# The opening of a diffusion layer on one core: the silu columns as a transfer of their own, another order of TensorE's first products, and one block of the third group moved by a place

## The chip, the core and the metric

The kernel runs on one core of one Trainium2 chip. The metric is the device time of one execution in microseconds (us); of the kernel before there are three runs, and their median stands for it.

## What is computed

One layer of a diffusion backbone, for 256 latent tokens with a prefix of 256 context tokens, width 2048, all in F32. What matters here is the first step, in which shift and scale come from a conditioning vector (`c` for the latent tokens, `c_ctx` for the context):

```python
def rms_norm(x, g):
    y = xf * lax.rsqrt(jnp.mean(xf * xf, axis=-1, keepdims=True) + EPS)
    return y * g
def modulate(x, g, shift, scale):
    return rms_norm(x, g) * (1 + scale) + shift
...
mod_x = jnp.split(jax.nn.silu(c) @ w_mod + b_mod, 6, axis=-1)
mod_c = jnp.split(jax.nn.silu(c_ctx) @ w_mod + b_mod, 6, axis=-1)
...proj(modulate(x, g_mix, mod_x[0], mod_x[1]))    # h @ w_in: the input projection
...proj(modulate(ctx, g_mix, mod_c[0], mod_c[1]))
```

Then follow windowed attention and a gated linear attention side by side, their merge, and a convolutional feed-forward; the change does not touch them.

## The kernel before

The projections multiply F32 by splitting each weight block into a high and a low part: ScalarE (ACT) copies the high part (`whi`, line 211), VectorE (DVE) takes the difference (`wlo`, line 212), and TensorE (PE) adds three products. The modulated tokens are split in the same way (`h00hi`, `h00lo` for the latent ones, `h10hi`, `h10lo` for the context).

The 16 tiles of 128 channels are worked in five groups (`GROUPS`: 2, 2, 4, 4 and 4 tiles), so that the projection can begin before the whole modulation is known. For each group, `mod_both` (line 312) makes the scale columns and then the shift columns: PE multiplies `cS`, the silu of the conditioning columns, with blocks of 1 MB of the modulation matrix (`pm <- mraw, cS`); DVE transposes the result (`mtr`); PE folds it into columns (`pcol <- mtr`), and DVE copies it out and adds the bias (lines 345 and 348). `affine_scale` and `affine_shift` apply the columns to the tokens.

The opening is a row of calls (lines 537 to 594). The constants come in two transfers on ACT's queue: `pack` (the identity matrix `ident`, biases, norm weights, the selector `sel` and, in its last 32 columns, both conditioning vectors), and `crow`. SP's queue loads the tokens (`xT`, two of 1 MB), the first group's four blocks, the first weights (`w_first`, four of 512 KB), the context tokens, and so on. `square_sums` squares the tokens on ACT and DVE, and PE adds them up over the channels with a matrix of ones (`pr <- sq, ones`: nine products, called by `add_up`). `factor_row` makes the norm's factors from that, three steps on DVE with two on ACT between. `idle(n)` issues n transposes of the identity matrix (`warm <- pack`), whose result nobody reads. `pe_seq` chains PE's instructions of the opening in the order of the calls.

The third group's blocks are worked among the second group's products. Six places are named by `mid()`: ahead of the second half of the latent QB projection, in its middle, behind it, in the middle of the KB projection, behind it, and in the middle of the VB projection. `steps` says how many blocks go to each place, `also` what else is done there, and `pend` holds the folding into columns that follows the last block of a kind. `kb` and `vb` are the sums of these projections over the groups, which DVE adds up from PE's banks (line 521).

PE's order follows the calls. On the other engines a scheduler places instructions by its own estimate of when they are ready. Each engine works in order.

## Time and profile before

| what | value |
|---|---|
| median of 3 runs | 1973.95 us (1973.88 to 1974.18) |
| the profiled execution's own time | 1973.72 us |
| its span, from the first instruction to the last | 1972.0 us |
| TensorE busy | 1952.8 us (99%) |
| VectorE busy | 1396.9 us (71%) |
| ScalarE busy | 971.6 us (49%) |
| DMA queue of SP | 413.45 MB, 63.7% of 16 engines' span |
| granted TensorE clock | 1.00 throughout |

A row of the timeline gives the start and the duration in us, the engine, the line, the operation, the tile that is written and the ones read, the shape and a count; in brackets stands how long the engine had been idle, and what ended that. SPq and ACTq are the queues that issue transfers. L83 and L95 are the helpers through which nearly all matmuls are issued, so the names of the tiles tell them apart.

### The profile page before, as it was taken

Reading aid. Unit: us, or ns where it says so; the run is one execution under the profiler, and the core shown is the slowest. Engines: PE = TensorE matmul, PEld = TensorE weight load, DVE = VectorE, ACT = ScalarE, POOL = GpSimd, SP = SyncE. Lnnn points to the kernel's source line nnn. Section 1 sums busy time; section 2 is a strip of 40 time slices with the busy share of each in tenths; the row PEclk is TensorE's granted clock in tenths of the full one; section 3 lists DMA queues with packets and bytes.
Section 4 is the critical chain, followed back from the end, with each engine's and each line's share of the span. In section 5 each row is a group of like instructions: output and inputs, shape, how many; then the busy total and the mean of one; then the engine's idle time right before and its main releaser. Section 6 shows DMA issues by size and latency. Waiting matters only on the chain.

```text
span 1972.0 us, 27091 instructions
## 1 busy us (share of the span) xinstructions
PE 1952.8 (99%) x10304; PEld 1635.6 (83%) x10304; DVE 1396.9 (71%) x2150; ACT 971.6 (49%) x1415; POOL 39.9 (2%) x60
## 2 busy tenths in 40 slices
PE   8999999999999999999999999999999999999999
PEld 6679988888887777888888888888888888888887
DVE  5756855785768998777776467989886545677754
ACT  5223655462346565444444445755555334555533
POOL 0010000020000000000000000000000000000000
PEclk9999999999999999999999999999999999999999
DMA  9975222226654466899997677688786556666563
GB/s 392 412 255 176 69 66 71 79 84 210 212 162 126 129 208 220 297 299 307 312 310 237 238 246 252 193 276 284 263 275 224 192 193 191 186 188 191 188 212 114
DMA packets 182867, 420.90 MB, mean 213 GB/s; under 512 B 12512, under 2 KB 12736, under 8 KB 177744
## 3 DMA queue, kind: packets, MB, share of 16 engines
q1 hardware_dynamic: 181200, 413.45, 63.7%
q0 software_dynamic: 1360, 5.54, 1.0%
q8 instruction: 81, 1.33, 0.3%
q14 instruction: 50, 0.41, 0.1%
q10 hardware_dynamic: 176, 0.17, 0.0%
HBM read 416.98 MB, written 2.13 MB: 213 GB/s over the span
## 4 chain that ended last, share of the span: by engine, by line
PE 94%; DVE 3%; ACT 1%; DMA 1%; issue 1%; ACTq 0%; DVEq 0%
PE acc L83 72%; PE accs L83 12%; PE pa L95 2%; PE poa L95 1%; PE pS L95 1%; PE po L95 1%; PE pm L95 1%; DVE wlo L212 1%; PE ptp L98 1%; DMA mraw<-in_w_mod 1%; ACT whi L211 0%; DVE q L831 0%; PE pto L98 0%; DMA pack<-in_k_pack 0%; DVE k L838 0%
## 5 line engine op out<-in xcount | busy, mean ns | idle before, releaser
L212 DVE TENSOR_TENSOR wlo<-raw,whi 128x1024 fp32r<-128x1024 f32 x568 | 694.0, 1223 | 426.5 <-ACT whi L211 387.8
L211 ACT ACTIVATE whi<-raw 128x1024 fp32r<-128x1024 f32 x568 | 601.1, 1059 | 785.1 <-PE acc L83 605.0
L83 PE MATMUL accs<-h,whi 128*128 128x512 f32 x704 | 176.3, 392 | 0.0
L83 PE MATMUL acc<-h,whi 128*128 128x512 f32 x640 | 160.4, 392 | 0.0
L83 PEld LDWEIGHTS accs<-h,whi 128*128 128x128 f32 x704 | 126.6, 189 | 22.6
L83 PE MATMUL acc<-whi,h01hi 128*128 128x512 f32 x352 | 139.7, 397 | 0.0
L83 PE MATMUL acc<-whi,h00hi 128*128 128x512 f32 x352 | 139.2, 395 | 0.0
L83 PE MATMUL acc<-whi,h01lo 128*128 128x512 f32 x352 | 138.4, 393 | 0.0
L83 PE MATMUL acc<-whi,h00lo 128*128 128x512 f32 x352 | 137.6, 391 | 0.0
L83 PE MATMUL acc<-whi,al 128*128 128x512 f32 x352 | 137.0, 389 | 0.0
L83 PE MATMUL acc<-whi,ah 128*128 128x512 f32 x352 | 137.0, 389 | 0.0
L83 PEld LDWEIGHTS acc<-h,whi 128*128 128x128 f32 x640 | 115.1, 189 | 20.6
L83 PEld LDWEIGHTS accs<-h,wlo 128*128 128x128 f32 x704 | 96.0, 190 | 6.9
L83 PE MATMUL acc<-wlo,h01hi 128*128 128x512 f32 x352 | 99.0, 396 | 0.0
L83 PE MATMUL accs<-h,wlo 128*128 128x256 f32 x704 | 98.2, 282 | 0.0
L83 PE MATMUL acc<-wlo,h00hi 128*128 128x512 f32 x352 | 98.1, 394 | 0.0
L83 PE MATMUL acc<-wlo,ah 128*128 128x512 f32 x352 | 94.3, 389 | 0.0
L83 PEld LDWEIGHTS acc<-h,wlo 128*128 128x128 f32 x640 | 87.4, 190 | 6.3
L83 PE MATMUL acc<-h,wlo 128*128 128x256 f32 x640 | 89.4, 282 | 0.0
L376 DVE CUSTOM_DVE_ANT_0 raw<-raw,csrow,pack 128x1024 f32<-128x1024 f32 x64 | 81.2, 1278 | 0.0
L83 PEld LDWEIGHTS acc<-whi,al 128*128 128x128 f32 x352 | 66.1, 188 | 13.7
L83 PEld LDWEIGHTS acc<-whi,ah 128*128 128x128 f32 x352 | 66.1, 188 | 13.7
(376 smaller groups left out, 3553.0 us busy)
## 6 DMA issues: line engine op xcount, KB each, us to landing
raw<-in_w_in SPq DMA_DIRECT2D x204, 512.0 KB, 4.5
raw<-in_w_up SPq DMA_DIRECT2D x176, 512.0 KB, 4.2
raw<-in_w_modT SPq DMA_DIRECT2D x128, 512.0 KB, 4.6
raw<-in_w_down SPq DMA_DIRECT2D x88, 512.0 KB, 3.6
mraw<-in_w_mod SPq DMA_DIRECT2D x30, 1024.0 KB, 12.5
raw<-in_w_attn_o SPq DMA_DIRECT2D x32, 512.0 KB, 5.3
raw<-in_w_gla_o SPq DMA_DIRECT2D x32, 512.0 KB, 5.4
raw<-in_w_out SPq DMA_DIRECT2D x32, 512.0 KB, 4.4
```

The costliest lines, as they stand in the source:

```text
L83: r = pe_seq(PE.matmul(*a, **k))
L95: return pe_seq(after(PE.matmul(*a, **k)))
L98: return pe_seq(after(PE.transpose(*a)))
L211: j = S.activation(hi[:, 0:n, :], raw[:, 0:n, :], AF.Copy).ins
L212: i = V.tensor_tensor(lo[:, 0:n, :], raw[:, 0:n, :], hi[:, 0:n, :].bitcast(F32), op=ALU.subtract).ins
L376: i0 = V.tensor_tensor_reduce(out=raws[i], in0=raws[i], in1=row[0], scale=1.0, scalar=d if h else bmod[:, b0:b0 + 1], op0=ALU.mult, op1=AL ...
```

## The change

It has five parts. The conditioning columns leave `pack` and become a transfer of their own, `ccol`, first in ACT's queue; `pack` goes behind `crow`. The opening has fewer idle transposes, and the first scale block (`a0`) goes ahead of the last three sums of squares. The last shift block of the first and the second group is loaded whole, no longer in halves. DVE's `gm1` is put behind the first square. Of the third group's four shift blocks three stay at the fourth place, and one goes to the fifth; its columns are folded at the sixth.

```diff
-    pack = cst.tile([P, 322], F32, name="pack")
-    nc.scalar.dma_start(pack, A["k_pack"])
+    ccol = cst.tile([P, KT, 2], F32, name="ccol")
+    nc.scalar.dma_start(ccol.rearrange("p k s -> p (k s)"), A["k_ccol"])
     crow = sm.tile([KT, P], F32, name="crow", tag="t128", bufs=2)
     nc.scalar.dma_start(crow, A["k_crow"])
+    pack = cst.tile([P, 290], F32, name="pack")
+    nc.scalar.dma_start(pack, A["k_pack"])
...
-    S.activation(cS[:, :, 0:2], pack[:, 290:322].rearrange("p (k s) -> p k s", s=2), AF.Silu)
+    S.activation(cS[:, :, 0:2], ccol, AF.Silu)
...
-            src = A["w_mod01"][part, t0 + k0 // nk].rearrange("p (c d) -> p c d", c=nk)
-            if t0 < 4 and part == 0 and k0:
-                load(raw[:, 0:nk // 2, :], src[:, 0:nk // 2, :])
-                load(raw[:, nk // 2:nk, :], src[:, nk // 2:nk, :])
-            else:
-                load(raw, src)
+            load(raw, A["w_mod01"][part, t0 + k0 // nk].rearrange("p (c d) -> p c d", c=nk))
...
-    idle(10)
+    idle(8)
     pr, add_up = square_sums(0)
     add_up(0, 6)
-    V.tensor_scalar(gm1, gmix, -0.5, None, op0=ALU.mult)
+    in_order(squared[0], V.tensor_scalar(gm1, gmix, -0.5, None, op0=ALU.mult).ins)
     (a0, a1, ea), (b0, b1, eb) = mods[0]
+    a0()
     add_up(6, 9)
     factor_row(pr)
-    a0()
-    idle(6)
     a1()
-    idle(4)
+    idle(2)
     ea()
     b0()
     affine_scale(0, *groups[0])
-    idle(6)
+    idle(4)
     b1()
...
-                steps = iter([1, 2, 1, 4, 0, 0])
+                steps = iter([1, 2, 1, 3, 1, 0])
...
-                also = iter([next_columns] * 3 + [scale_2, next_columns, lambda: affine_shift(0, *groups[2])])
+                def shift_2():
+                    next_columns()
+                    affine_shift(0, *groups[2])
+
+                also = iter([next_columns] * 3 + [scale_2, next_columns, shift_2])
```

The start of ACT's queue before, from the program's first row on (`ACT_TABLE_LOAD` loads the table for silu, then the one for logarithm and exponential):

```order
L116 DMA pack<-in_k_pack 128x322
L118 DMA crow<-in_k_crow 16x128
L133 ACT_TABLE_LOAD
L133 ACTIVATE cS<-pack 128x16x2
L134 ACTIVATE crow<-crow 16x128
```

And with the change:

```order
L116 DMA ccol<-in_k_ccol 128x32
L118 DMA crow<-in_k_crow 16x128
L120 DMA pack<-in_k_pack 128x290
L135 ACT_TABLE_LOAD
L135 ACTIVATE cS<-ccol 128x16x2
L136 ACTIVATE crow<-crow 16x128
```

The transfer that PE's first instruction reads, pack, has moved from the first place to the third; ccol has as many rows as pack had.

PE's opening before, up to the last idle transposes (`pm1` are scale products, `pm0` shift products):

```order
L538 MATMUL warm_109<-pack_81 128x128
L535 MATMUL warm_109<-pack_81 128x128 x10
L462 MATMUL pr_121<-sq_122,ones_91 128x256 x4
L462 MATMUL pr_121<-sq_124,ones_91 128x256 x2
L462 MATMUL pr_121<-sq_127,ones_91 128x256
L462 MATMUL pr_121<-sq_131,ones_91 128x256 x2
L95 MATMUL pm1_0_152<-mraw_153,cS_93 32x256 x8
L535 MATMUL warm_109<-pack_81 128x128 x6
L95 MATMUL pm1_0_152<-mraw_169,cS_93 32x256 x8
L535 MATMUL warm_109<-pack_81 128x128 x4
L95 MATMUL pcol1_0_185<-mtr_179,pack_81 32x16
L95 MATMUL pm0_0_192<-mraw_193,cS_93 32x256 x8
```

And with the change:

```order
L537 MATMUL warm_111<-pack_85 128x128
L534 MATMUL warm_111<-pack_85 128x128 x8
L461 MATMUL pr_121<-sq_122,ones_93 128x256 x4
L461 MATMUL pr_121<-sq_124,ones_93 128x256 x2
L95 MATMUL pm1_0_141<-mraw_142,cS_95 32x256 x8
L461 MATMUL pr_121<-sq_127,ones_93 128x256
L461 MATMUL pr_121<-sq_131,ones_93 128x256 x2
L95 MATMUL pm1_0_141<-mraw_163,cS_95 32x256 x8
L534 MATMUL warm_111<-pack_85 128x128 x2
L95 MATMUL pcol1_0_177<-mtr_173,pack_85 32x16
L95 MATMUL pm0_0_184<-mraw_185,cS_95 32x256 x8
```

The first scale block has moved ahead of the last three sums; behind the second scale block two idle transposes are left of four, and between the scale blocks none. Behind these rows stand four idle transposes instead of six, then the last shift block, as before.

DVE around the third group's shift columns before, from the scaling of the context tokens on:

```order
L502 SCALAR_TENSOR_TENSOR xr_87<-xr_87,scale_102,rrow 128x256 x4
L335 STREAM_TRANSPOSE mtr<-pm_4_693 128x512
L521 TENSOR_TENSOR kb_107<-kb_107,acc 128x512 x4
L345 COPY shift_101<-pcol_4_740 32x2x4 x4
L348 TENSOR_TENSOR shift_101<-shift_101,pack 128x2x4
L212 TENSOR_TENSOR wlo<-raw,whi 128x1024
L512 SCALAR_TENSOR_TENSOR h00lo<-xr_85,shift_101,h00hi 128x256 x4
L521 TENSOR_TENSOR vb_108<-vb_108,acc 128x512 x4
```

And with the change:

```order
L501 SCALAR_TENSOR_TENSOR xr_89<-xr_89,scale_104,rrow 128x256 x4
L520 TENSOR_TENSOR kb_109<-kb_109,acc 128x512 x4
L332 STREAM_TRANSPOSE mtr<-pm_4_681 128x512
L342 COPY shift_103<-pcol_4_752 32x2x4 x4
L520 TENSOR_TENSOR vb_110<-vb_110,acc 128x512
L214 TENSOR_TENSOR wlo<-raw,whi 128x1024
L345 TENSOR_TENSOR shift_103<-shift_103,pack 128x2x4
L520 TENSOR_TENSOR vb_110<-vb_110,acc 128x512
L511 SCALAR_TENSOR_TENSOR h00lo<-xr_87,shift_103,h00hi 128x256 x4
L520 TENSOR_TENSOR vb_110<-vb_110,acc 128x512 x2
```

The transpose has moved behind the kb evictions, and between the copies of the shift columns and their bias add (L348 before, L345 now) stand a vb eviction and a weight split; one more eviction stands ahead of h00lo.

More of the change, by code (lines that the diff above doesn't have):

```diff
@@ L429, in layer_kernel @@
     vb0 = M("vb0", [P, 4, 512])
+    squared = []
     def square_sums(s):
@@ L442, in square_sums @@
             else:
-                V.tensor_tensor(q, x_, x_, op=ALU.mult)
+                squared.append(V.tensor_tensor(q, x_, x_, op=ALU.mult).ins)
                 parts.extend(q[:, k, :] for k in range(4))
@@ L1348 @@
         [consts.pop("k_ident")] + [col(data.pop(n)[0]) for n in ("b_mod", "g_mix", "g_ffn")]
-        + [consts.pop("k_sel"), np.stack([col(c), col(c_ctx)], axis=2).reshape(P, 2 * KT)], axis=1)
+        + [consts.pop("k_sel")], axis=1)
+    data["k_ccol"] = np.stack([col(c), col(c_ctx)], axis=2).reshape(P, 2 * KT)
     conv = data.pop("conv_w")[0]
```

## The prediction

> **What bounds the kernel now.** I read the page first, then the waits of TensorE (PE), then the order of time in two short stretches. The page says that there is almost nothing to gain: PE is busy for all but 19.2 us of the span, and the chain that ended last is PE for 94%.

> ```profile
> span 1972.0 us, 27091 instructions
> PE 1952.8 (99%) x10304; PEld 1635.6 (83%) x10304; DVE 1396.9 (71%) x2150; ACT 971.6 (49%) x1415; POOL 39.9 (2%) x60
> PE 94%; DVE 3%; ACT 1%; DMA 1%; issue 1%; ACTq 0%; DVEq 0%
> ```

> Who kept PE waiting, longest in total first (us in total, times, longest):

> ```profile
> PE warm L538 <- DMA pack<-in_k_pack: 6.7, 1, 6.7
> PE pm L95 <- DMA mraw<-in_w_mod: 1.2, 1, 1.2
> ```

> So PE's two waits on transfers are the wait for the constants at the start (6.7) and one wait for a block of the modulation matrix (1.2). The change touches both. Beside them the opening holds padding: "warm" transposes that compute nothing and count as busy. The opening in order of time, PE only (start, duration, operation; a matmul of 256 columns in F32 stands as two records):

> ```profile
> 6.68 0.47 PE L538 MATMUL warm<-pack 128*128 128x128 f32 x1 [6.68 <-DMA pack<-in_k_pack]
> 6.95 2.34 PE L535 MATMUL warm<-pack 128*128 128x128 f32 x10
> 9.08 3.63 PE L462 MATMUL pr<-sq,ones 128*128 128x256 f32 x12
> 13.07 1.64 PE L462 MATMUL pr<-sq,ones 128*128 128x256 f32 x6 [0.37 <-DVE sq L453]
> 14.64 1.07 PE L95 MATMUL pm<-mraw,cS 128*32 128x256 f32 x16
> 19.14 0.87 PE L535 MATMUL warm<-pack 128*128 128x128 f32 x6
> 19.94 1.07 PE L95 MATMUL pm<-mraw,cS 128*32 128x256 f32 x16
> 20.94 0.66 PE L535 MATMUL warm<-pack 128*128 128x128 f32 x4
> 23.30 0.39 PE L83 MATMUL acc<-h00hi,whi 128*128 128x256 f32 x1 [0.46 <-ACT h00hi L511]
> ```

> The first real product starts at 23.30; from there PE hardly stops, so a shift of that moment reaches the end unless a later wait swallows it. The last shift block is the 512 KB load of this row, issued in the stretch 6.6 to 7.0 us:

> ```profile
> mraw<-in_w_mod SPq DMA_DIRECT2D x1, 512.0 KB, 12.8
> ```

> It lands at about 19.5. Its products started only at 19.94, since six warm transposes stood ahead (19.14 to 20.0). From that start to the first product are 3.36 us (19.94 to 23.30).

> **The change, part 1: the opening.** With four warm transposes in place of six the last block's products could start on landing, and the first product come at 19.5 + 3.36 = 22.9, **0.4 earlier**. That holds only if PE gets there in time, and PE's very first instruction reads pack. Pack was first in ACT's queue and is now third. These are its issue and that of crow, the landing times (us from issue), and the packets that each queue started between 3 and 5 us (q1 is SP's queue, q10 ACT's; two rows of the queue table, then ACT's):

> ```profile
> q1 hardware_dynamic: 82, 0.67, 80.1%
> q10 hardware_dynamic: 82, 0.11, 16.0%
> ```

> ```profile
> 0.74 0.41 ACTq L116 DMA_DIRECT2D pack<-in_k_pack  x1
> 1.18 0.45 ACTq L118 DMA_DIRECT2D crow<-in_k_crow  x1
> ```

> ```profile
> pack<-in_k_pack ACTq DMA_DIRECT2D x1, 161.0 KB, 5.9
> crow<-in_k_crow ACTq DMA_DIRECT2D x1, 8.0 KB, 5.9
> ```

> 82 against 82: the engines serve the two queues one packet each in turn, whatever the size. 82 turns on 16 engines in 2.0 us make 0.39 us a turn, nearly all of it SP's packet. Pack has 128 rows, 8 turns on each engine; so has ccol, although it is a tenth of the size. I therefore put ccol where pack was, a little sooner for its smaller packets (a packet of pack takes 16.0% x 16 x 2.0 / 82 = 0.06, so 8 of them save 0.5 at most; I take 0.3): 6.3 instead of 6.6. Crow landed 0.5 after pack (1.18 + 5.9 against 0.74 + 5.9) and keeps that: 6.8. Pack then needs 8 turns of its own, 3.1: **9.9**, 3.2 later than now. Bounds: 7.1, when crow landed as the last of the same bytes, if bytes decide and not turns; and 10.5 with nothing saved on ccol and one more turn to close. I take 9.9, since the row comes from this very queue beside this very stream.

> [...]

> Now PE from 9.9 on. Nine warm transposes by the two rows (0.27, then 0.213 each): 2.0, until 11.9. Six sums of squares are 12 records. Their weight loads tell the speed:

> ```profile
> 8.87 2.16 PEld L462 LDWEIGHTS pr<-sq,ones 128*128 128x128 f32 x8
> 11.57 0.73 PEld L462 LDWEIGHTS pr<-sq,ones 128*128 128x128 f32 x4 [0.55 <-DVE sq L447]
> ```

> Eight took 2.16, later four 0.73: about three of the first eight still ran at half speed, so PE doubled its speed some 3.3 us after it began. After the change the same: 12 x 0.22 plus 3 x 0.21 = 3.3, until 15.2. The first scale block, now ahead of the last three sums, takes 1.07 (row 14.64), until 16.3; the three sums 1.4 (row 13.07, 1.64 less waits), until 17.7. They ended at 14.7 before. Behind them hangs the row of factors on VectorE (DVE):

> ```profile
> 14.75 0.42 DVE L471 TENSOR_SCALAR vrow<-pr 128x256 f32<-128x256 f32 x1 [1.22 <-PE pr L462]
> 16.57 0.43 DVE L475 TENSOR_TENSOR vrow<-vrow 128x256 f32<-128x256 f32 x1
> 17.59 0.45 DVE L335 STREAM_TRANSPOSE mtr<-pm 128x256 f32<-128x256 f32 x1
> 21.08 0.45 DVE L335 STREAM_TRANSPOSE mtr<-pm 128x256 f32<-128x256 f32 x1 [0.75 <-PE pm L95]
> ```

> From vrow to the end of L475 are 2.25, so 17.7 becomes 19.95; the transpose of the scale columns now follows at once, 0.45: 20.4; pcol on PE 20.5. Everything behind pcol waits with it on PE: the first shift block 1.07 (21.55), four warm transposes 0.65 (22.2), the last shift block, which has long landed. From its start 3.36: first product at **25.5, 2.2 later**. Had pack landed at 7.1, it would be 22.9; above that each microsecond of pack is one of the first product, so the upper bound is 26.1.

> At no cost: gm1 behind the first square (0.17 on DVE, which then idles for ACT's squares); whole blocks for halves (the same bytes); silu some 0.3 sooner, and with it ACT's squares, for which PE no longer waits. The third load of w_first now waits for pack's semaphore, at 9.9 not 9.0; the blocks queued ahead last until 19.5. Were that cover gone, it would cost the 0.9.

> **Part 2: the third group.** PE and then DVE and ACT around the second wait:

> ```profile
> 62.56 2.74 PE L95 MATMUL pm<-mraw,cS 128*32 128x512 f32 x21
> 66.52 1.07 PE L95 MATMUL pm<-mraw,cS 128*32 128x512 f32 x8 [1.22 <-DMA mraw<-in_w_mod]
> 69.61 0.25 PE L95 MATMUL pcol<-mtr,pack 128*32 128x32 f32 x2
> 69.79 0.50 PE L83 MATMUL acc<-whi,h00hi 128*128 128x512 f32 x1
> 73.55 1.07 PE L83 MATMUL acc<-wlo,h00hi 128*128 128x512 f32 x4
> 75.45 1.06 PE L95 MATMUL pm<-mraw,cS 128*32 128x512 f32 x8
> 76.45 0.39 PE L83 MATMUL acc<-h00hi,whi 128*128 128x256 f32 x1
> ```

> ```profile
> 70.69 0.66 DVE L345 COPY shift<-pcol 32x8 f32<-32x8 f32 x4
> 71.38 0.17 DVE L348 TENSOR_TENSOR shift<-shift,pack 128x8 f32<-128x8 f32 x1
> 71.51 1.23 DVE L212 TENSOR_TENSOR wlo<-raw,whi 128x1024 fp32r<-128x1024 f32 x1
> 72.66 1.67 DVE L512 SCALAR_TENSOR_TENSOR h00lo<-xr,shift,h00hi 128x256 fp32r<-128x256 f32 x4
> 74.24 2.47 DVE L521 TENSOR_TENSOR vb<-vb,acc 128x512 f32<-128x512 f32 x4
> ```

> ```profile
> 71.58 1.71 ACT L511 ACTIVATE h00hi<-xr,shift 128x256 fp32r<-128x256 f32 x4
> ```

> The fourth block moves behind 2.1 us of products (67.59 to 69.7), where it has landed: the wait of **1.22 goes**. But its pcol moves from ahead of the VB products to their middle, and what hangs on it comes late. If PE were not shifted otherwise, VB would start at 68.35, pcol at 72.1, the copies end at 73.1. Then, by DVE's new order, the bias add no longer follows at once: one vb eviction (2.47/4 = 0.6) and a wlo (1.14) stand ahead, so it ends at 75.0. ACT's first h00hi ends at 75.5, DVE's first two h00lo at 76.05 and 76.45. PE would be ready for the third group's first product at 75.2 and has its fourth operand pair only at 76.5, where it stood at 76.9 before (0.46 after 76.45). So **0.85 of the 1.22 is given back** by a new wait; bounds for it are 0, if the add finds its place early, and 1.2.

> **Sum.** Both count from the profiled execution, 1973.72 us (span 1972.0 plus 1.7 around it), 0.23 under the median. With the opening 2.2 later the old 1.22 wait would have vanished by itself: PE arrives after the block. The end shifts by 2.2 - 1.22 + 0.85 = **+1.8**: 1975.5 against 1973.72, **1975.8** against the median. The load stream is no brake: the block that PE waited for is the only one it ever waited for behind 23.3.

> **Rivals.**
> [...]
> [...]
> - Slower beyond the bound: PE stays at half speed through all twelve records of the sums, which it would if it doubled only after 7 us of work, at 17 us. They then take 12 x 0.43 = 5.2 and not 3.3: +1.9 on top, 1977.7, and 1978.3 with pack at 10.5. The rows show 3.3 us once; the moment may differ when the start does. [...]

> **How the numbers follow.** Pack late: 0.54, 1974.4 to 1976.8 by pack at 9.3 to 10.5 and the new wait at 0 to 1.2. Pack early: 0.20. Early without the new wait: 0.12. Half speed for longer: 0.09. Something that I don't see: 0.05. The first three make the range 1972.2 to 1977.3. What a measurement of this kernel can tell from no change is about 0.2%, here 3.9 us, and none but the slow clock reaches it: same 0.92, slower 0.06, faster 0.02.

> **What would show it.** PE's first wait on pack: 9.9 (7 would be the first rival). First product near 25.5. No wait of pm on mraw near 65. The third group's first products waiting for ACT's h00hi and DVE's h00lo, 0.85 in all. I am wrong if pack lands by 8, if the sums of squares end before 15, or if the first product is earlier than 23.3.

## The result and the profile after

| kernel | median | executions | ratio to before |
|---|---|---|---|
| before | 1973.95 us | 1973.55 to 1974.49, 20 | |
| changed | 1977.62 us | 1976.89 to 1978.21, 20 | 1.0018 [1.0012, 1.0024] |

The change makes the kernel 3.7 us slower (the interval of the ratio is 2.4 to 4.7 us). The forecast had the sign and 1.8 us. Its remark that a measurement of this kernel can tell no less than 3.9 us from no change was too pessimistic: the two sets of twenty don't overlap. The profiled execution took 1977.10 us, with a span of 1975.3.

The page of the changed kernel reads like the one before:

```profile
span 1975.3 us, 27065 instructions
PE 1953.1 (99%) x10292; PEld 1635.4 (83%) x10292; DVE 1397.2 (71%) x2150; ACT 971.1 (49%) x1415; POOL 39.9 (2%) x60
PE 94%; DVE 4%; ACT 1%; issue 1%; DMA 0%; ACTq 0%; DVEq 0%
```

PE is busy for 0.3 us longer, with 12 instructions fewer, and it idles 22.2 us in place of 19.2. Who kept it waiting, in the changed kernel (chosen rows; us in total, times, longest):

```profile
PE warm L537 <- DMA pack<-in_k_pack: 9.7, 1, 9.7
PE pcol L95 <- DVE mtr L332: 1.7, 2, 1.3
PE acc L83 <- ACT h10hi L510: 0.7, 1, 0.7
PE acc L83 <- ACT h00hi L510: 0.7, 2, 0.5
```

The wait for pack has grown from 6.7 to 9.7; the wait of `pm` for `mraw` is gone. Of the two waits of `pcol` for the transpose one, of 1.3, is new (the other, of 0.4, was there before), and so is the second wait for `h00hi`, of 0.2. The two DMA queues between 3 and 5 us (packets started, MB, share of 16 engines):

```profile
q1 hardware_dynamic: 102, 0.84, 98.8%
q10 hardware_dynamic: 102, 0.01, 4.1%
```

Again SP's queue and ACT's started the same number of packets, although ACT's are now those of the small ccol. The opening of PE in the changed kernel, in order of time:

```profile
9.69 0.47 PE L537 MATMUL warm<-pack 128*128 128x128 f32 x1 [9.69 <-DMA pack<-in_k_pack]
9.96 1.91 PE L534 MATMUL warm<-pack 128*128 128x128 f32 x8
11.66 4.50 PE L461 MATMUL pr<-sq,ones 128*128 128x256 f32 x12
16.09 1.07 PE L95 MATMUL pm<-mraw,cS 128*32 128x256 f32 x16
17.09 1.56 PE L461 MATMUL pr<-sq,ones 128*128 128x256 f32 x6
18.58 1.07 PE L95 MATMUL pm<-mraw,cS 128*32 128x256 f32 x16
21.35 0.20 PE L95 MATMUL pcol<-mtr,pack 128*32 128x16 f32 x1 [1.32 <-DVE mtr L332]
26.34 0.38 PE L83 MATMUL acc<-h00hi,whi 128*128 128x256 f32 x1 [0.46 <-ACT h00hi L510]
```

The twelve records of the first six sums take 4.50 us, 0.375 each; the later six, 0.26 each. The trace records the granted clock's first change, to full, at 15.19, and the records ahead of it are the slow ones. That is 5.50 us after PE's first instruction. In the kernel before it came at 10.00, 3.32 after the first instruction. (The 1.00 "throughout" in the table of the kernel before, and the clock column of the stretches below, count the time ahead of the first recorded change as full; the records say otherwise: an idle transpose takes 0.213 among the eight at 9.96 and 0.117 among the eight at 24.79 (1.09 us in all). This slower pace is what I call half clock in the opening; the value 0.50 itself the trace records only in later stretches.) The first product comes at 26.34, 3.04 later than before (23.30).

To see where the time stays, I took the start of each of PE's 9504 products of the projections and of attention in one trace and subtracted that of the same product before. The columns are places of the kernel before, in us of its trace (an ordinary table, worked out from the two traces):

| profiled kernel | first product, 23.3 | 42 | 44.3 | 73.6 | 77 | end | own time |
|---|---|---|---|---|---|---|---|
| changed | +3.04 | +3.04 | +3.03 | +1.87 | +2.84 | +3.33 | 1977.10 |
| changed, second profile (after_again) | +2.66 | +2.67 | +4.19 | +3.03 | +3.99 | +4.25 | 1978.01 |
| before, second profile (before_again) | +0.02 | +0.03 | +0.03 | +0.42 | +0.42 | +0.73 | 1974.44 |
| place_alone (see below) | +0.15 | +0.15 | +1.67 | +0.50 | +1.47 | +1.67 | 1975.40 |
| place_back (see below) | +2.35 | +2.36 | +3.89 | +2.55 | +2.55 | +2.97 | 1976.74 |

The third row is the measure of what a single profile is worth: two profiles of one kernel drift apart by 0.7 us over the span. The first row loses some 0.5 us behind 77, where the two profiles of before differ by 0.3. The second row holds something that the first doesn't: 1.5 us that are lost between 42 and 44.3.

### The profile page after: what moved, and what is told of

The parts are those of the page before. It is cut to its first block, busy times and chain, and to the rows that moved or that the text cites. A ratio compares the mean times of both kernels' runs of the same rounds, so it can differ in the third digit from the quotient of the medians.

```text
span 1975.3 us, 27065 instructions
## 1 busy us (share of the span) xinstructions
PE 1953.1 (99%) x10292; PEld 1635.4 (83%) x10292; DVE 1397.2 (71%) x2150; ACT 971.1 (49%) x1415; POOL 39.9 (2%) x60
## 4 chain that ended last, share of the span: by engine, by line
PE 94%; DVE 4%; ACT 1%; issue 1%; DMA 0%; ACTq 0%; DVEq 0%
PE acc L83 72%; PE accs L83 12%; PE pa L95 2%; PE poa L95 1%; PE pm L95 1%; PE pS L95 1%; PE po L95 1%; DVE wlo L214 1%; PE ptp L98 1%; DMA pack<-in_k_pack 0%; ACT whi L213 0%; DVE q L833 0%; PE pto L98 0%; PE pr L461 0%; DVE k L840 0%
## 5 line engine op out<-in xcount | busy, mean ns | idle before, releaser
L83 PE MATMUL accs<-h,whi 128*128 128x512 f32 x704 | 176.3, 392 | 0.0
L83 PE MATMUL acc<-h,whi 128*128 128x512 f32 x640 | 160.4, 392 | 0.0
L83 PEld LDWEIGHTS accs<-h,whi 128*128 128x128 f32 x704 | 126.6, 189 | 22.6
L83 PE MATMUL acc<-whi,h01hi 128*128 128x512 f32 x352 | 139.7, 397 | 0.0
L83 PE MATMUL acc<-whi,h00hi 128*128 128x512 f32 x352 | 139.2, 395 | 0.0
L83 PE MATMUL acc<-whi,h01lo 128*128 128x512 f32 x352 | 138.4, 393 | 0.0
L83 PE MATMUL acc<-whi,h00lo 128*128 128x512 f32 x352 | 137.7, 391 | 0.0
L83 PE MATMUL acc<-whi,al 128*128 128x512 f32 x352 | 137.0, 389 | 0.0
L83 PE MATMUL acc<-whi,ah 128*128 128x512 f32 x352 | 137.0, 389 | 0.0
L83 PEld LDWEIGHTS acc<-h,whi 128*128 128x128 f32 x640 | 115.1, 189 | 20.6
L83 PEld LDWEIGHTS accs<-h,wlo 128*128 128x128 f32 x704 | 96.0, 190 | 6.9
L83 PE MATMUL acc<-wlo,h01hi 128*128 128x512 f32 x352 | 99.0, 396 | 0.0
L83 PE MATMUL acc<-wlo,h00hi 128*128 128x512 f32 x352 | 98.3, 395 | 0.0
L83 PE MATMUL accs<-h,wlo 128*128 128x256 f32 x704 | 98.2, 282 | 0.0
L83 PE MATMUL acc<-wlo,ah 128*128 128x512 f32 x352 | 94.4, 389 | 0.0
L83 PEld LDWEIGHTS acc<-h,wlo 128*128 128x128 f32 x640 | 87.4, 190 | 6.3
L83 PE MATMUL acc<-h,wlo 128*128 128x256 f32 x640 | 89.4, 282 | 0.0
L83 PEld LDWEIGHTS acc<-whi,h00hi 128*128 128x128 f32 x352 | 66.4, 188 | 14.0 <-ACT whi L213 0.8
L83 PEld LDWEIGHTS acc<-whi,al 128*128 128x128 f32 x352 | 66.1, 188 | 13.7
## 6 DMA issues: line engine op xcount, KB each, us to landing
raw<-in_w_in SPq DMA_DIRECT2D x204, 512.0 KB, 4.6
raw<-in_w_up SPq DMA_DIRECT2D x176, 512.0 KB, 4.1
raw<-in_w_modT SPq DMA_DIRECT2D x128, 512.0 KB, 4.5
raw<-in_w_down SPq DMA_DIRECT2D x88, 512.0 KB, 3.6
raw<-in_w_attn_o SPq DMA_DIRECT2D x32, 512.0 KB, 5.3
raw<-in_w_gla_o SPq DMA_DIRECT2D x32, 512.0 KB, 5.3
raw<-in_w_out SPq DMA_DIRECT2D x32, 512.0 KB, 4.7
```

The lines of the kernel that those rows point to most:

```text
L83: r = pe_seq(PE.matmul(*a, **k))
```

## The experiments

### Which part of the change costs

Four kernels, beside before at 1973.93. **consts_back** is the changed kernel with the constants' transfers as before, **consts_alone** the kernel before with these alone changed:

```diff
-    pack = cst.tile([P, 322], F32, name="pack")
-    nc.scalar.dma_start(pack, A["k_pack"])
+    ccol = cst.tile([P, KT, 2], F32, name="ccol")
+    nc.scalar.dma_start(ccol.rearrange("p k s -> p (k s)"), A["k_ccol"])
     crow = sm.tile([KT, P], F32, name="crow", tag="t128", bufs=2)
     nc.scalar.dma_start(crow, A["k_crow"])
+    pack = cst.tile([P, 290], F32, name="pack")
+    nc.scalar.dma_start(pack, A["k_pack"])
...
-    S.activation(cS[:, :, 0:2], pack[:, 290:322].rearrange("p (k s) -> p k s", s=2), AF.Silu)
+    S.activation(cS[:, :, 0:2], ccol, AF.Silu)
...
```

**place_alone** is the kernel before with the third group's block moved, **place_back** the changed kernel without that:

```diff
-                steps = iter([1, 2, 1, 4, 0, 0])
+                steps = iter([1, 2, 1, 3, 1, 0])
...
```

> The changed kernel with the constants as before (conditioning columns inside pack, pack first in ACT's queue), all else changed. Theory (the late pack is the whole cause): TensorE starts at 6.7 instead of 9.7, its first product comes at about 22.9 instead of 26.3, and the third group's place is worth 0.2; 1973.3 us. Rival (TensorE's new order, with the scale block ahead of the last sums, is the cause): the row of factors still comes late, first product at 25 or later, 1976 us or more.

> The kernel before with only the constants changed (ccol, crow, pack in ACT's queue). Theory: TensorE starts at 9.7, the first product comes at about 26.5, the old wait of 1.2 for the modulation block vanishes because TensorE comes after it; 1976.1 us. Rival (TensorE's new order is the cause): first product near 23.5, 1974 us.

> The kernel before with only the third group's fourth shift block moved to the fifth place. Theory (the wait of 1.2 goes, a wait of 1.0 for the shift columns comes): 1973.7 us, and in the trace no wait for mraw near 65, but one for ACT's h00hi near 75. Rival (the new wait belongs to the late opening and not to the place): the full 1.2 is saved, 1972.7 us.

> The changed kernel with the fourth shift block back at the fourth place. Theory (after the late opening nothing waits for the block any more, so the move only costs its new wait of 1.0): 1976.6 us. Rival (the move still saves its 1.2): 1978.8 us.

| run | median (range, 11 executions) | ratio to before | first product | first change to full clock |
|---|---|---|---|---|
| consts_back | 1973.57 (1972.94 to 1974.51) | 0.9998 [0.9989, 1.0007] | 22.89 | 11.59 |
| consts_alone | 1976.07 (1975.34 to 1976.88) | 1.0011 [1.0002, 1.002] | 24.99 | 12.62 |
| place_alone | 1973.75 (1973.55 to 1975.4) | 1.0002 [0.9993, 1.001] | 23.45 | 11.83 |
| place_back | 1976.24 (1975.6 to 1976.8) | 1.0012 [1.0003, 1.0021] | 25.66 | 13.69 |

The loss needs the late constants: with them as before it is gone, and by themselves they make 2.1 us of it. (The time of consts_alone is as expected, but partly by luck: its first product came at 24.99 and not near 26.5, and 1.2 us were then lost near 43, in a stretch of which more below.)

The moved block is worth 0.2: in place_alone the products stand 1.67 later than before at 44.3 and 1.47 at 77, and consts_back and both profiles of the changed kernel show the same difference of 0.2. Where the opening is late and the block stays at its old place, 1.34 goes over that stretch (place_back from 3.89 to 2.55), since PE then comes after the block has landed. So behind a late opening the moved block costs some 1.1, and taking it back alone recovers 1.4 of the 3.7 (place_back, 1976.24). The old wait for the block was a reserve that took up earlier delays; the move spent it.

The new wait stands on DVE, here in the changed kernel:

```profile
75.53 0.67 DVE L342 COPY shift<-pcol 32x8 f32<-32x8 f32 x4 [2.35 <-PE pcol L95]
76.23 0.69 DVE L520 TENSOR_TENSOR vb<-vb,acc 128x512 f32<-128x512 f32 x1
76.83 1.22 DVE L214 TENSOR_TENSOR wlo<-raw,whi 128x1024 fp32r<-128x1024 f32 x1
77.97 0.16 DVE L345 TENSOR_TENSOR shift<-shift,pack 128x8 f32<-128x8 f32 x1
```

The bias add waits 1.8 us for an eviction and a weight split that nothing at this place needs.

### The clock of the opening

If the half clock makes the loss, a PE that is brought to full clock while pack is still under way must win it back, with pack as late as ever. **fast_clock** does that with matmuls of the matrix of ones, which needs no transfer:

```diff
-    opening[:] = [pe_seq(PE.transpose(warm[:, 0:P], ident, ident)).ins]
+    opening[:] = [pe_seq(PE.matmul(warm[:, 0:64], ones, ones[:, 0:64], start=True, stop=True)).ins]
+    for _ in range(45):
+        pe_seq(PE.matmul(warm[:, 0:64], ones, ones[:, 0:64], start=True, stop=True))
+    idle(1)
     idle(8)
```

> The changed kernel with 46 matmuls of the matrix of ones with itself (64 columns, result unread) at PE's very start, so that PE works from about 3 us on while pack is still on its way. Pack, its landing and every later instruction stay as they are. Theory: of the 3.04 us by which the first product came later than before, the lateness of pack alone accounts for little, since the sums' records ran 4.50 us at half clock; with the clock up by about 10 us the sums end about 2.4 earlier, the last shift block's landing (18.5) becomes the limit or nearly so, the first product comes at 22 to 24, and the time is near 1974 (up to 1.5 more in executions with a second half-clock stretch). Rival: the lateness of pack is the cause and the clock is not; then the first product stays near 26.3 and the time near 1977.

It took 1988.96 us (1986.14 to 1989.21, 5 executions; ratio 1.0073 [1.006, 1.0085]), and the first product came at 36.89. Neither theory had that. PE in fast_clock:

```profile
1.54 19.41 PE L539 MATMUL warm<-ones 128*128 128x64 f32 x90
20.74 2.13 PE L534 MATMUL warm<-pack 128*128 128x128 f32 x9
22.66 4.06 PE L461 MATMUL pr<-sq,ones 128*128 128x256 f32 x12
```

A record of 64 columns takes 0.216 us, as long as an idle transpose of 128 columns at half clock (0.213). So the 46 matmuls last until 20.95, 11 us beyond pack's landing. And the clock went up only at 25.28: 19.7 us of a PE without a gap did not raise it, while 3.3 us of records with 128 and 256 columns had done so in the kernel before. In these runs it did not suffice that PE always had an instruction; the width of the instructions decided (with 128 columns, in wide_clock, the clock is full at 5.60).

**wide_clock** is the same with all 128 columns and 26 matmuls:

```diff
-    opening[:] = [pe_seq(PE.transpose(warm[:, 0:P], ident, ident)).ins]
-    idle(8)
+    opening[:] = [pe_seq(PE.matmul(warm[:, 0:P], ones, ones, start=True, stop=True)).ins]
+    for _ in range(25):
+        pe_seq(PE.matmul(warm[:, 0:P], ones, ones, start=True, stop=True))
+    idle(9)
```

> The changed kernel with 26 matmuls of the matrix of ones with itself, all 128 columns, on PE from about 1 us to about 10 us, while pack is on its way (0.43 each at half clock, 0.25 at full clock); pack, the nine idle transposes that read it and all behind stay. It is the run fast_clock again, whose 64 columns did not raise the clock. Theory (the clock is decided at the end of windows of 3.41 us, by the share of a window in which PE streams): the clock is full by 4.4 to 7.9 us, the sums' twelve records take 2.6 to 3.3 instead of 4.50, the first product comes at 24.3 to 24.9 instead of 26.34, no second half-clock stretch falls on the gaps near 42 us, and the time is 1974.9 to 1975.8. Rival (pack's lateness alone made the 3.04): the first product stays at 26.0 or later and the time at 1976.9 or more.

Measured: 1974.05 us (1973.86 to 1975.65, 11), beside before at 1974.05 and the changed kernel at 1977.86; ratio to before 1.0002 [0.9993, 1.0011]. The clock was full at 5.60. PE in wide_clock:

```profile
1.65 7.63 PE L539 MATMUL warm<-ones 128*128 128x128 f32 x50
9.59 1.20 PE L534 MATMUL warm<-pack 128*128 128x128 f32 x9 [0.31 <-DMA pack<-in_k_pack]
10.63 2.76 PE L461 MATMUL pr<-sq,ones 128*128 128x256 f32 x12
15.81 1.07 PE L95 MATMUL pm<-mraw,cS 128*32 128x256 f32 x16
23.21 0.39 PE L83 MATMUL acc<-h00hi,whi 128*128 128x256 f32 x1 [0.46 <-ACT h00hi L510]
```

Pack is as late as in the changed kernel (9.6), yet the first product comes at 23.21, 3.13 earlier, and 0.09 earlier than before the change. The nine transposes take 1.20 and the twelve records 2.76 (4.50). So with a full clock the late pack no longer costs anything against the kernel before. In its times the theory held, and was too timid: I had expected 24.3 at the earliest. That the clock is decided at the end of windows, by the share in which PE streams, this run does not show; the last section has what the traces say of it.

It does not follow that the clock alone is to blame. pack_on_sp (below) has pack early and its twelve records mostly at half clock, 4.71 in all, and loses nothing either; in consts_back they take 4.35. The first six sums end at 13.4 in wide_clock, at 12.8 in pack_on_sp and at 16.2 in the changed kernel. Only a late pack and the slow clock together push the sums so far back that the first product waits for them; to mend either is enough.

### The second half-clock stretch

The profiles of consts_alone, place_alone and place_back show the clock at half again for 3.41 us, 30.72 us after it first went full. Here are the stretch (second row) and the same length ahead of it (first row), in the second profile of the changed kernel (us, busy time of each engine with its instructions, granted clock, DMA share, GB/s):

```profile
core 0: us, PE busy (x) PEld busy (x) DVE busy (x) ACT busy (x) POOL busy (x), PEclk, DMA share, GB/s
...
41.58:44.99 3.41, 2.18 (x17) 1.59 (x14) 3.12 (x14) 0.91 (x2) 0.00 (x0) 1.00 1.07 405
44.99:48.41 3.42, 3.42 (x25) 1.93 (x24) 1.72 (x6) 0.00 (x0) 0.00 (x0) 0.50 1.01 416
```

And in place_alone:

```profile
39.13:42.55 3.42, 2.19 (x17) 1.67 (x14) 3.13 (x14) 0.91 (x2) 0.00 (x0) 1.00 1.05 386
42.55:45.96 3.41, 3.41 (x24) 1.92 (x23) 1.76 (x5) 0.00 (x0) 0.00 (x0) 0.50 1.06 407
```

The changed kernel's first profile, at the same distance from its first change (15.19 + 30.72 = 45.91), and no stretch follows:

```profile
42.50:45.91 3.41, 2.53 (x17) 2.14 (x18) 3.12 (x14) 0.91 (x2) 0.00 (x0) 1.00 1.08 418
45.91:49.32 3.41, 3.41 (x33) 2.40 (x32) 2.25 (x9) 1.09 (x2) 0.00 (x0) 1.00 1.01 416
```

PE was busy for 64% of the 3.41 us ahead of the stretch, and for 74% where none followed. What it waits for there, in the second profile of the changed kernel:

```profile
42.20 0.24 PE L95 MATMUL pcol<-mtr,pack 128*32 128x16 f32 x2 [0.43 <-DVE mtr L332]
43.10 0.38 PE L83 MATMUL acc<-h10hi,whi 128*128 128x256 f32 x1 [0.67 <-ACT h10hi L510]
```

These are the gaps around the folding of the context tokens' scale columns. They are in the kernel before as well (0.37 and 0.67). The two profiles of the changed kernel differ in the moment of the first change, 14.27 with the stretch and 15.19 without it; I took it that this moment decides whether the gaps cost 1.5 us. Two controls and two kernels with idle transposes in these gaps:

```diff
     b0()
+    idle(4)
     ea()
+    idle(8)
     affine_scale(0, *groups[1])
```

**before_again** and **after_again** are the two kernels unchanged; **after_filled** has this edit on the changed kernel, **clock_filled** on wide_clock.

> The kernel before, unchanged, as a control beside the others. Theory: 1973.9, within 0.5; no execution at a mean granted clock of 0.999, and no half-clock stretch behind the opening. Rival: the second half-clock stretch near 42 us belongs to the chip and comes in this kernel too; then some executions stand 1.3 to 1.6 above the rest.

> The changed kernel, unchanged, for a second profile and eleven more times. Theory: the phase of the 3.41 us windows against the kernel's start differs from execution to execution; the first step to full clock comes 2.9 to 6.1 after PE's start, and where it comes between about 12.9 and 14.7 the profile has a second half-clock stretch 30.72 later (none at 15.2 and above); the times spread over 1976.4 to 1978.3. Rival: the moment belongs to the kernel; then the step is at 15.2 again, without a second stretch, and the times lie within 0.3 of each other.

> The changed kernel with idle transposes in the waits that PE has around the folding of the context tokens' scale columns (4 ahead of it, 8 behind it; about 39 to 43 us). Theory: the second half-clock stretch of 3.41 us, which some executions show near 42 us, follows from PE's waits in the 3.41 us ahead of it; with those waits filled no execution has it, all stand at 1976.3 to 1977.3 (the upper of the two groups of the changed kernel is gone). Rival: the stretch comes from elsewhere, and the executions still fall into two groups more than 0.5 apart, 1977 and 1978.

> The run wide_clock with idle transposes in PE's gaps around the folding of the context tokens' scale columns (4 ahead of it, 8 behind it). Theory: the upper times of wide_clock (1975.26 to 1975.65, 3 of 11) are executions whose window fell on these gaps and were followed by 3.41 us at half clock; with the gaps filled no time is above 1974.8, and the rest stays at 1973.8 to 1974.5 (the fillers themselves cost up to 0.2). Rival: the upper times have another cause, and about 3 of 11 still stand 1.2 or more above the lowest.

| run | median (range, 11 executions) | ratio to before | profile: full clock at | second stretch |
|---|---|---|---|---|
| before_again | 1974.13 (1973.47 to 1974.9) | 1.0 [0.9991, 1.0009] | 10.17 | none |
| after_again | 1977.86 (1976.96 to 1978.1) | 1.0019 [1.001, 1.0027] | 14.27 | 44.99 to 48.41 |
| after_filled | 1976.88 (1975.65 to 1977.8) | 1.0014 [1.0005, 1.0022] | 15.74 | none |
| clock_filled | 1974.04 (1973.84 to 1974.79) | 1.0001 [0.9993, 1.001] | 6.38 | none |

after_again came out as the theory had it: the first change at 14.27 and no longer at 15.19, the second stretch 30.72 later, the times spread over 1.1 us. That rules out a moment that belongs to the kernel. In before_again the median held, but five of its eleven executions have a mean granted clock of 0.999, which I had taken as the mark of the stretch: the end of the program at half clock lowers the mean too (in the first profile of the changed kernel it takes 0.9 us, and with 2 us in all the mean rounds to 0.999), so that mark is not safe, and whether the kernel before ever has the stretch stays open.

Its times can't show it: place_alone, the same kernel but for the moved block, has four of eleven executions at 1975.10 to 1975.40, some 1.4 above the rest, and a stretch in its profile, while none of the 151 executions of the kernel before is above 1974.93. The wait of 1.22 for the block, which place_alone no longer has, would take most of such a loss back, as it does in place_back.

after_filled missed its range on both sides, and its times were wider, still in two groups (1975.65 to 1975.99, and from 1976.76 on). The median is 1.0 under that of after_again, and the slowest, 1977.8, is the profiled one, whose first change came latest of all (15.74, with pack as late as 10.61). Spread of the first change and spread from the second stretch are mixed there. clock_filled separates them: no time above 1974.79, where wide_clock had 3 of 11 at 1975.26 to 1975.65. PE in clock_filled, about where the gaps were:

```profile
40.00:43.40 3.40, 3.40 (x32) 2.93 (x34) 3.11 (x13) 0.82 (x2) 0.00 (x0) 1.00 1.06 388
```

Three of eleven against none is thin taken alone; with the rows above I hold these gaps for the cause, which is argued more than shown.

### Whether the opening can be made good

**warm_on_ones** is the changed kernel with all idle transposes replaced by matmuls of ones with 64 columns:

```diff
-            pe_seq(PE.transpose(warm[:, 0:P], ident, ident))
+            pe_seq(PE.matmul(warm[:, 0:64], ones, ones[:, 0:64], start=True, stop=True))
...
```

**wide_free** has 16 matmuls of ones with 128 columns in place of the first nine only, and DVE's `gm1`, which reads pack, behind the last square (`squared[1]`, a new entry):

```diff
...
-    in_order(squared[0], V.tensor_scalar(gm1, gmix, -0.5, None, op0=ALU.mult).ins)
+    in_order(squared[1], V.tensor_scalar(gm1, gmix, -0.5, None, op0=ALU.mult).ins)
```

**add_first** is wide_free with the bias add (`added_last`) forced ahead of the first vb eviction:

```diff
...
+            if first and i == 0:
+                in_order(added_last[0], j)
...
```

**free_filled** is wide_free with its gaps filled, and with the edit of clock_filled:

```diff
-    add_up(0, 6)
+    add_up(0, 4)
+    for _ in range(7):
+        pe_seq(PE.matmul(warm[:, 0:P], ones, ones, start=True, stop=True))
+    add_up(4, 6)
...
-    idle(2)
+    idle(8)
...
```

**pack_on_sp** is the changed kernel with one edit; SP's queue begins with this transfer:

```diff
-    nc.scalar.dma_start(pack, A["k_pack"])
+    nc.sync.dma_start(pack, A["k_pack"])
```

> The changed kernel with every idle transpose of the identity matrix replaced by a matmul of the matrix of ones with itself (64 columns, result unread), so that PE needs pack for nothing until the scale columns (pcol). Theory: with PE's start no longer bound to pack, the opening is bound by the last shift block, which lands near 18.5; the first product comes 3.36 later, at 21.9 to 22.2, and the time is 1972.3 to 1973.3. Rival: the order of the scale block ahead of the last three sums costs by itself (the row of factors on DVE starts later); then the first product is not ahead of 23.3 and the time is 1974 or more.

> The changed kernel with 16 such matmuls of ones in place of the nine idle transposes at the start, and DVE's gm1 (which reads pack) behind the last sum of squares of the first tokens in place of behind the first: neither PE nor DVE needs pack before the scale columns. Theory: nothing of the opening waits for pack or runs at half clock for long; the last shift block, which lands near 18.4, is the limit, the first product comes at 21.7 to 22.3, and with the new wait of the third group (1.0 against 1.22 saved) the time is 1972.2 to 1973.0, under the kernel before by 1 to 1.7. Rival: the order of the scale block ahead of the last three sums holds up the row of factors; then the first product is behind 23.3 and the time 1973.9 or more.

> The run wide_free with one more edit: DVE is made to do the bias add of the third group's shift columns ahead of the first vb eviction. Theory: the new wait of 1.0 in front of the third group's first product goes, and the time is 0.7 to 1.0 under wide_free's. Rival: the evictions that now come later hold PE's banks and give it back; then the time is within 0.3 of wide_free's.

> The run wide_free with its three gaps filled: 7 matmuls of ones between the fourth and the fifth sum of squares, 8 idle transposes in place of 2 behind the second scale block, and the 4 and 8 of clock_filled. Theory: wide_free's two times at 1975.75 and 1975.94, of which one is profiled with two half-clock stretches, go; all times lie at 1972.8 to 1973.5, under every time of the kernel before. Rival: a filler too many delays the sums or the folding, and the median is 1973.6 or more.

> The changed kernel with pack's transfer first on SP's queue, ahead of the tokens, and all else as in the change. Theory: pack lands at 3.5 to 5, PE starts there and has its full clock by 11 at the latest, before most of the sums; the load stream is 0.3 to 0.5 later for pack's 145 KB, so the first product comes at 22.1 to 22.8, and the times are 1972.8 to 1973.8 with some up to 1975.2 (executions with a second half-clock stretch). Rival: the change's own order in the opening (the scale block ahead of the last sums, fewer idle transposes) leaves PE's windows too thin and the clock comes late all the same; then the first product is behind 24 and the median at 1975 or more.

| run | median (range, 11 executions) | before beside it | ratio | first product |
|---|---|---|---|---|
| warm_on_ones | 1974.52 (1973.63 to 1975.35) | 1974.11 | 1.0002 [0.9993, 1.0011] | 24.05 |
| wide_free | 1973.18 (1973.0 to 1975.94) | 1974.05 | 0.9998 [0.9989, 1.0007] | 23.66 |
| add_first | 1973.22 (1973.11 to 1976.26) | 1974.05 | 0.9999 [0.999, 1.0008] | 22.14 |
| free_filled | 1973.87 (1973.58 to 1977.86) | 1973.88 | 1.0002 [0.9994, 1.0011] | 23.36 |
| pack_on_sp | 1973.60 (1973.03 to 1974.23) | 1973.88 | 0.9999 [0.999, 1.0008] | 22.97 |

warm_on_ones missed: PE in it waits for no pack, but its 64 columns don't raise the clock (the first change is at 12.72), and the twelve records, with short waits for squares among them, took longer than ever:

```profile
6.85 5.93 PE L461 MATMUL pr<-sq,ones 128*128 128x256 f32 x12 [1.69 <-DVE sq L442]
```

wide_free's median is 0.9 under before, just short of the 1 to 1.7 that was expected. Nine of its eleven executions lie at 1973.00 to 1973.28, under the lowest of before beside it (1973.62), but with the other two its interval doesn't tell it from no change. One of those two was profiled: 1975.75, 2.6 above the median. In it the sums' wait for a square leaves PE busy for 1.57 of 3.42 us, and the clock is at half for the 3.41 us behind them:

```profile
10.77 1.52 PE L463 MATMUL pr<-sq,ones 128*128 128x256 f32 x4 [1.85 <-DVE sq L446]
12.22 1.93 PE L95 MATMUL pm<-mraw,cS 128*32 128x256 f32 x16
```

```profile
7.96:11.38 3.42, 1.57 (x8) 1.06 (x7) 1.10 (x2) 3.41 (x4) 0.59 (x1) 1.00 1.03 431
11.38:14.79 3.41, 3.41 (x21) 1.40 (x20) 1.40 (x4) 0.51 (x1) 0.00 (x0) 0.50 1.01 425
```

The same scale block takes 1.93 here and 1.07 at full clock. So a clock that was won early was lost again here, right behind a gap of 1.85; that the gap is the cause is argued from this one profile. free_filled closed the gaps, and its median was 0.7 worse, as its rival had it: in its profile the last shift block landed only at 19.95, and PE waited 0.96 for it. Why that transfer was later there (it landed at 18.47 in wide_free, but at 19.81 in wide_clock), and what made one execution 1977.86, is not settled.

add_first fell to its rival. The wait for the third group's columns is gone, and another has come, for a bank that vb's next eviction, now later, has to free:

```profile
74.54 0.38 PE L83 MATMUL acc<-h00hi,whi 128*128 128x256 f32 x1
...
76.44 0.39 PE L83 MATMUL acc<-h00hi,whi 128*128 128x256 f32 x1 [0.53 <-DVE vb L674]
```

pack_on_sp is the plain cure, but not by the way that was expected:

```profile
3.09 0.47 PE L537 MATMUL warm<-pack 128*128 128x128 f32 x1 [3.09 <-DMA pack<-in_k_pack]
8.08 4.71 PE L461 MATMUL pr<-sq,ones 128*128 128x256 f32 x12 [2.81 <-DVE sq L442]
22.97 0.38 PE L83 MATMUL acc<-h00hi,whi 128*128 128x256 f32 x1 [0.46 <-ACT h00hi L510]
```

Pack lands at 3.04, but PE then waits 2.81 for the first square, and the clock is full only at 11.88, where 11 at the latest was expected. The first sums run as slowly as in the changed kernel, only 3.6 earlier, and that is enough: the first product comes at 22.97 (a little later than expected), and no execution is above 1974.23. So the changed order of the opening is no worse than the one before, once pack is there early. None of the five is faster than before by what this measurement can tell.

## Why the prediction was off, step by step

- **Pack at 9.9**: right. It landed at 9.64. The equal packet counts came again (102 and 102, with 0.84 MB against 0.01). The chances of 0.20 and 0.12 and the lower end of the range, 1972.2, stood on a pack that lands near 7 behind two other transfers. No run shows that; PE's first wait for it ended at 9.69 here, at 9.83 in the second profile and at 10.61 in after_filled.
- **"PE doubled its speed some 3.3 us after it began. After the change the same"**: this step failed. It was 5.50 in one profile of the changed kernel and 4.44 in the other. In the profiles of the other kernels that start on pack from ACT's queue, the delay runs from 2.94 (consts_alone) to 5.20 (consts_back); with pack on SP's queue it was 8.79. I had taken one trace's moment for a constant. The sums' records took 4.50 and not 3.3. They began 0.2 sooner than forecast, and what is behind them came 0.85 to 0.9 later: sums until 18.6 (forecast 17.7), pcol at 21.35 (20.5), first product at 26.34 (25.5). The first product was off by 0.84 in this profile and by 0.46 in the other.
- **"Each microsecond of pack is one of the first product"**: right in the changed kernel only because PE starts cold on pack. With PE already at full clock (wide_clock), pack's 3 us cost nothing against the kernel before. The term of 2.2 was a price of both together, the late transfer and the slow clock behind it. Some price of the wait alone is left: add_first, whose PE needs pack for nothing that early, has its first product at 22.14, 1.07 ahead of wide_clock's.
- **The third group**: right. The wait of 1.22 went; 0.97 was given back by the bias add behind an eviction and a split (forecast 0.85, bounds 0 and 1.2). Together -0.2 where I had -0.37.
- **What I did not see**: the second half-clock stretch. It costs 1.5 (from 2.67 to 4.19 in the second profile), and the sum had no term for it. In 21 of the changed kernel's 31 executions the mean granted clock is 0.999; these took 1977.47 to 1978.21, the other ten 1976.89 to 1977.23. Two such groups fit an extra 1.5 that many executions have, with an earlier first change against it. Which execution has it is seen only in the two that were profiled. The profiled one without it, 1977.10, lies within the 1977.3 of the forecast; the median, 1977.62, lies beyond it. So of the miss of 1.8 the moment of the clock made 0.84 and the third group some 0.2; the rest is, as far as the two groups show it, this stretch, beside the drift of about 0.5 behind 77.
- **The rival with the slow clock** (0.09) had the mechanism and the doubt, and put it as if the alternative were half speed through all twelve records. The time it gave, 1977.7, is that of the median, but by another sum: 4.50 and not 5.2 for the records, and 1.5 from a place that it did not know. That the time fits is luck. I had named the possibility that the moment differs, and counted it as a remote case, where it made the moment of the clock an unknown term, with bounds of its own, in the likeliest case as well; the range ended at 1977.3 for want of it.

## What to carry to other kernels

At the start of a kernel, ask of PE's first stretch not only what it waits for but at which clock it runs. The full clock came 4.44 and 5.50 us after PE's start in two profiles of one kernel, and 2.94 to 5.50 after it over nine profiles of kernels that start alike; where the opening is bound by PE, this variation reaches the first product (26.34 and 25.96 in those two). A transfer that PE's first instruction needs is best early (pack_on_sp, 1973.60), or PE is given dense work of 128 columns that needs no transfer (wide_clock, 1974.05; the changed kernel beside it 1977.86). Gaps of 1.2 us in all may have cost another 1.5 by the clock behind them. And a wait is also a reserve (in place_back it took up 1.34): what removes it lets earlier delays through to the end.

## What the runs showed of the chip

The moment of the first change differs between two executions of one kernel: 15.19 and 14.27. The change's whole effect was 0.2%, and most of it hung on the clock. Where the clock fell near 42 us, PE had waited for 1.2 us in the window ahead, never for a whole one.
